# Residual updates in two token halves, weight casts ordered after the put-backs, and a rotary key of 128 rows in a one-layer FFN, mixer and FFN kernel

## The chip, the cores and the metric

The kernel runs on one core of a Trainium2 chip. The metric is device time in microseconds (us), lower is better. Engines are named as the profile names them: PE (TensorE matmul) and PEld (its weight loads), DVE (VectorE), ACT (ScalarE), POOL (GpSimd) and SP (SyncE, whose queue issues nearly all DMAs).

## The reference, cut

One encoder layer in float32 on 256 tokens of width 2048. D_FF is 5632; the attention has 8 heads, with 128 columns of a head's own key and a rotary key of 64 columns that all heads share.

```python
mod = silu(c) @ w_ada + b_ada                      # nine vectors: shift, scale, gate, three times
n = rms(h, ffn1_norm) * (1 + sc1) + sh1
h = h + 0.5 * g1 * ((silu(n @ w_gate) * (n @ w_up)) @ w_down)          # FFN 1
n = rms(h, mix_norm) * (1 + sc2) + sh2
proj = n @ w_in                                    # u, v, c_q, c_kv, k_pe
a = gmlp_mixer(u, v)
m = mla_mixer(c_q, c_kv, k_pe)                     # scores = q_nope . k_nope + q_pe . k_pe
h = h + g2 * (concat[rms(a), rms(m)] @ w_out)      # mix
n = rms(h, ffn2_norm) * (1 + sc3) + sh3
h = h + 0.5 * g3 * ((silu(n @ w_gate) * (n @ w_up)) @ w_down)          # FFN 2
h = rms(h, final_norm)
```

## The kernel before

**Weights.** Every weight matrix comes through `split`: one DMA of 128 x 2048 into a `raw` tile; then, for each of its two halves, ACT copies a rounded high part `whi` (128x1024, L170) and DVE subtracts it to form the low part `wlo` (L174). The matmuls (all of them are recorded at L121, in the helper `mm`) take hi x hi, hi x lo and lo x hi products, where activations are split alike (`nh`, `nl`). One step is one `raw` tile: for each half of it 8 matmuls with `whi` and 4 with `wlo`, 24 in all, over two PSUM banks of 128 tokens x 512 columns, one bank for each half of the tokens. There are buffers for five raw tiles and for four hi and four lo halves.

**FFN.** `ffn` runs a first part (12 column groups `pg`, each with gate and up columns) and a second part, each followed by its down projection. In the first part the rows of the contraction are taken in passes: FFN 1 in row groups of 3, 3, 3, 3 and 4 tiles (`grouped`), FFN 2 in passes of two, one and one blocks (`in_passes`). Between passes the partial sums of a column group are copied out of PSUM by ACT (`keep_part`, L362), and at its next pass put back into two fresh banks by ACT (`take_part`, L366), which I call the put-back. After the last pass ACT and DVE form silu(g) * u (`th` at L326, `sg` and `a` at L327 and L328); four PE transposes (`tps`, L239) flip it, ordered after the last matmul of a step; ACT (L350) and DVE (L351) write the hi and lo parts of `s`.

**Order.** The kernel is written in program order, and each engine works through its own queue in the order in which the code issues; a helper `tc.issue_after` puts what stands in its block behind a named instruction, and where it isn't used, a scheduler settles the order of independent work. `run` begins step i+1 (`begin`: new banks, put-back, `split`) while the matmuls of step i are written.

**Down projection and boundaries.** Four column blocks c of 512 columns. At the end of a block `add_out` multiplies the two banks by the gate row (L290), adds the product to the residual `h` (L291), and `TokenNorm.add` sums squares on ACT (L252). `gate_row` forms the gate of 512 columns by four transposes (`tpg`) and an ACT copy (L284), once in each column block during the first half of an FFN. After the last block `TokenNorm.done` reduces the sums (L259), keeps PE going with matmuls called `idle`, and takes the root by a power on POOL (L182); `make` then normalizes (`hn`, L268), transposes (`tpn`) and writes the hi and lo parts of `n` (L276 to L278) for the next stage. The same stands behind the mixer's out projection. At the end the output is written by four DMAs of 512 columns for all tokens (L1011).

**Scores.** The rotary key `kpeT` holds the same 64 rows twice, at rows 0 and 64; `scores` takes for each head the 64 rows that its query stands in.

Of the kernel before, what the change touches and what calls it, by code (L numbers as in the profile page):

```python
# [17 lines left out]
P = 128  # L18
D = 2048
# [51 lines left out]
def encoder_layer(ctx: ExitStack, tc: tile.TileContext, outx, *, xT, x, pos, cst, vnorm, w_ada, gu1k, gu1, dn1a,  # L71
# [171 lines left out]
    class TokenNorm:  # L243


        def __init__(self):
            self.ss = stat(8)

        def add(self, c):
            for t in range(2):  # L250
                sq = tmp.tile([P, 512], F32, tag="hn", bufs=2, name="sq")
                act.activation(sq, h[:, t, c * 512 : c * 512 + 512], AF.Square, scale=1.0 / math.sqrt(D),  # L252
                               accum_out=self.ss[:, t * 4 + c : t * 4 + c + 1])

        def done(self, warm=False):
            ss = stat(2)
            if warm:
                keep_warm(mark["gu"], 6)
            dve.tensor_reduce(ss, self.ss.rearrange("p (t c) -> p t c", t=2), axis=AX.X, op=ALU.add)  # L259
            if warm:  # L260
                idle = bank("aux", "idle")
                keep_warm(mm(idle[:, :2], ident, ss, True, True), 6)
            self.r = rstd(ss, 2)

        def make(self, n, d0, sh, gs):
            hn = tmp.tile([P, 2, T], F32, tag="hn", bufs=2, name="hn")
            for t in range(2):
                dve.tensor_scalar(hn[:, t], h[:, t, d0 * P : d0 * P + T], self.r[:, t : t + 1], None, op0=ALU.mult)  # L268
            ps = bank("aux", "tpn")
            flip4(ps, lambda j, t: hn[:, t, j * P : j * P + P])  # L270
            for j in range(2):
                d = d0 + j
                nr = tmp.tile([P, T], F32, tag="nr", name="nr")
                s, g = mods[:, sh, d : d + 1], mods[:, gs, d : d + 1]
                o = ps[:, j * T : j * T + T]
                act.activation(n[0][:, d], o, AF.Identity, bias=s, scale=g)  # L276
                dve.tensor_scalar(nr, o, g, s, op0=ALU.mult, op1=ALU.add)  # L277
                dve.tensor_tensor(n[1][:, d], nr, n[0][:, d].bitcast(F32), op=ALU.subtract)  # L278

    def gate_row(m, c, g):  # L280
# [5 lines left out]
    def add_out(banks, c, g, norm=None):  # L286
        sl = slice(c * 512, c * 512 + 512)
        for t in range(2):
            e = tmp.tile([P, 512], F32, tag="hn", bufs=2, name="e")
            dve.tensor_tensor(e, banks[t], g, op=ALU.mult)  # L290
            dve.tensor_tensor(h[:, t, sl], h[:, t, sl], e, op=ALU.add)  # L291
        if norm:
            norm.add(c)
# [10 lines left out]
    def wide(w, banks, xs, first, last):  # L304

        half = (len(xs) + 1) // 2
        for i, ((whi, wlo), x) in enumerate(zip(w, (xs[:half], xs[half:]))):
            hi, lo = (y.rearrange("p (k c) -> p k c", k=len(x)) for y in (whi, wlo))
            for k, (a, b) in enumerate(x):
                for t in range(2):  # L310
                    mm(banks[t], a[:, token(t)], hi[:, k], first and i == 0 and k == 0, False)
                    mm(banks[t], b[:, token(t)], hi[:, k], False, False)
            for k, (a, _) in enumerate(x):
                for t in range(2):
# [3 lines left out]
    def gu_chunk(w, banks, n, kt0, nk, first, last):  # L318
        wide(w, banks, [(n[0][:, kt], n[1][:, kt]) for kt in range(kt0, kt0 + nk)], first, last)
# [11 lines left out]
    def ffn(gu, dn, n, gate, ada_pg, ada_dn, lead, groups, prep, norm, before_down=None):  # L331
        with tc.tile_pool(name="actp", bufs=1) as actp, tc.tile_pool(name="ftmp", bufs=2) as ftmp:
# [3 lines left out]
            grow = ftmp.tile([P, 4, 512], F32, bufs=1, name="grow")  # L336
# [31 lines left out]
            def run(steps, part, slots):  # L368
# [14 lines left out]
                for i, (pg, kt0, nk, opens, load, more) in enumerate(steps):  # L383
                    gu_chunk(w, banks, n, kt0, nk, kt0 == 0, kt0 + nk == KT)
# [10 lines left out]
            def in_passes(slots):  # L395
                def load(pg, kg):
# [4 lines left out]
                     for kgs in PASSES for pg in range(FIRST) for kg in kgs], {}, slots)  # L401
# [48 lines left out]
            for half in range(2):  # L450
# [5 lines left out]
                kqs = len(slots) // 4  # L456
                for c in range(4):
                    banks = [bank("acc" if c % 2 else "aux", "dn") for _ in range(2)]
                    for kq in range(kqs):
                        if half == 0 and before_down:  # L460
# [3 lines left out]
                        wide(w, banks, slots[kq * 4 : kq * 4 + 4], kq == 0, kq == kqs - 1)  # L464
# [63 lines left out]
    rb1 = tmp.tile([P, T], F32, bufs=1, name="rb1")  # L528
# [50 lines left out]
    ffn(gu1, (dn1a, dn1b), n1, G1, ADA_UP1, ADA_DOWN1, gu1k, [gu1g[f"gu1_{g}"] for g in range(len(GROUPS))], prep1, norm, gate_cols(G1))  # L579
# [3 lines left out]
    norm2.done(True)  # L583
    n2 = new_n()
    with tc.tile_pool(name="mix", bufs=1) as mix:
        u = mix.tile([P, 2, 1024], F32, name="u")
        vg = mix.tile([P, 2, 1024], F32, name="vg")
        cqT = mix.tile([P, 2, 4, T], F32R, tag="cm", name="cqT")
        ckvT = [mix.tile([P, 2, T], F32R, tag="qT", bufs=2, name="ckvT") for _ in range(2)]
        kpeT = mix.tile([P, T], F32, name="kpeT")  # L590
# [6 lines left out]
        def a_form(w, banks, lhs, kts, first, last):  # L597
            per = len(kts) // 2
            for half in range(2):
                hi, lo = (x.rearrange("p (k c) -> p k c", k=per) for x in w[half])  # L600
                ks = kts[half * per : half * per + per]
                for i, kt in enumerate(ks):
                    for t in range(2):
# [3 lines left out]
                for i, kt in enumerate(ks):  # L607
                    for t in range(2):
# [3 lines left out]
        def proj(i, kg, banks, n_ada, prep=False):  # L612
            if prep:
                for d in (kg * 4, kg * 4 + 2):
                    norm2.make(n2, d, SH2, SC2)
            w = split(win_a[i, kg])
            ada(n_ada)
            a_form(w, banks, n2, list(range(kg * 4, kg * 4 + 4)), kg == 0, kg == 3)
# [18 lines left out]
        def rotate(dst, x, heads):  # L637
# [3 lines left out]
            ps = tmp.tile([P, 4, 64 * heads], F32, tag="hn", bufs=2, name="ps")  # L641
            p1, p2, p3, p4 = (ps[:, i].rearrange("p (t a b) -> p t a b", t=2, a=heads) for i in range(4))
# [57 lines left out]
        for kg in range(4):  # L700
            proj(1, kg, banks, ADA_MIX["v0"][kg])
            if kg == 1:
# [3 lines left out]
                act.copy(kpeT, ps[:, :T])  # L706
# [154 lines left out]
        def a_flip():  # L861
            mA = nslot.tile([P, KT, T], F32R, tag="nl", name="mA")
            transpose_split(u, 8, (mA[:, :8], mA[:, 8:]), "out_norm_gmlp")
            return mA
# [5 lines left out]
        def scores(g, j):  # L870
            rows = slice(64 * j, 64 * j + 64)
# [34 lines left out]
        def out_pair(part, i, m, norm=None):  # L906
# [3 lines left out]
            if kq == 0:  # L910
                held[0] = [bank("acc", "wo") for _ in range(2)]
                held[1] = mix.tile([P, 512], F32, tag="grow", name="grow")
                gate_row(G2, c, held[1])
            ks = range(kq * 4, kq * 4 + 4)
            wide(w, held[0], [(m[:, k], m[:, 8 + k]) for k in ks], kq == 0, kq == 1)
            if kq:
                add_out(held[0], c, held[1], norm)
# [32 lines left out]
        mM = nslot.tile([P, KT, T], F32R, tag="nh", name="mM")  # L950
        for k in range(8):
# [3 lines left out]
            act.activation(mM[:, k], hr, AF.Identity, scale=g)  # L955
            dve.scalar_tensor_tensor(mM[:, 8 + k], hr, g, mM[:, k].bitcast(F32), op0=ALU.mult, op1=ALU.subtract)
        out_pair(0, 6, mA)
        out_pair(0, 7, mA)
        norm = TokenNorm()
        for dp in range(8):  # L960
# [5 lines left out]
    norm3.done(True)  # L966
    n3 = new_n()
# [8 lines left out]
    def prep3(kg, pg):  # L976
        if pg == 0 and kg < cut:
            for d in (kg * 4, kg * 4 + 2):
                norm3.make(n3, d, SH3, SC3)
        for m, d in ahead3.get((kg, pg), ()):  # L980
            mod_col(m, d, 1, True)
            if m == SH3:
                mod_end(SC3, d, d + 1, "scale", "ffn2_norm")
                mod_end(SH3, d, d + 1, "shift")
                if d % 2:
                    norm3.make(n3, d - 1, SH3, SC3)

    norm = TokenNorm()
    ffn(gu2, (dn2a, dn2b), n3, G3, none, (none, none), None, None, prep3, norm, gate_cols(G3))


    fn = const.tile([P, D], F32, tag="cb", name="fn")
    sync.dma_start(fn, fnorm)
    with tc.tile_pool(name="fin", bufs=1) as fin:
        o = fin.tile([P, 2, D], F32, name="o")
        for c in range(3):
            for t in range(2):
                sl = slice(c * 512, c * 512 + 512)
                dve.tensor_tensor(h[:, t, sl], h[:, t, sl], fn[:, sl], op=ALU.mult)
        norm.done()  # L1000
        for c in (3, 0, 1, 2):
            sl = slice(c * 512, c * 512 + 512)
            for t in range(2):
                r = norm.r[:, t : t + 1]
                if c == 3:
                    dve.scalar_tensor_tensor(o[:, t, sl], h[:, t, sl], r, fn[:, sl], op0=ALU.mult, op1=ALU.mult)
                elif c == 0 or (c == 1 and t == 0):
                    act.activation(o[:, t, sl], h[:, t, sl], AF.Identity, scale=r)
                else:
                    dve.tensor_scalar(o[:, t, sl], h[:, t, sl], r, None, op0=ALU.mult)  # L1010
            sync.dma_start(outx[:, :, sl], o[:, :, sl])  # L1011
# [93 lines left out]
```

## Time and profile before

| | |
|---|---|
| runs | 1840.97 us median of 3 (1837.91 to 1841.42) |
| the profiled execution | 1839.86 us, of which the span (first to last instruction) 1838.1 us |
| PE busy | 1788.3 us, 97% of the span |
| PEld / DVE / ACT / POOL busy | 1474.0 / 1329.1 / 964.8 / 29.4 us |
| mean granted TensorE clock | 0.989 of full speed |
| read from memory | 480.01 MB, 262 GB/s over the span |

A busy time is the sum of an engine's instructions; matmuls overlap in the pipeline, so the time from one start to the next is shorter than a record's own length (0.39 us for a matmul that starts 0.23 after the one before it). The releaser of a wait is the instruction that came last among those waited for.

### The profile page before, as it was taken

What the parts mean: (1) busy time and instruction counts of PE and PEld (TensorE: products, weight loads), DVE (VectorE), ACT (ScalarE), POOL (GpSimd) and SP (SyncE); (2) the same over time, 40 slices, a digit from 0 to 9 for tenths busy, and PEclk for the clock granted to TensorE, in tenths of its full rate; (3) what the DMA queues carried; (4) which work ended last, traced back from release to release, by engine and by line L of the source; (5) the groups of instructions that cost most, each with busy time, mean ns of one, the idle gap of its engine ahead of it and who ended that gap; (6) DMA issues with size and microseconds to landing.
All of it is one profiled execution on the core that took longest, in us unless ns stands there. A gap on an engine that the chain in (4) does not pass through costs nothing.

```text
span 1838.1 us, 21587 instructions
## 1 busy us (share of the span) xinstructions
PE 1788.3 (97%) x8078; PEld 1474.0 (80%) x8078; DVE 1329.1 (72%) x1730; ACT 964.8 (52%) x1456; POOL 29.4 (2%) x25
## 2 busy tenths in 40 slices
PE   6999999999999999999999999999999999999996
PEld 4788777888888888888877878888778888888885
DVE  7888878887777778696877886666687855555554
ACT  3788865343444444366675544467654334444442
POOL 1000000000000000001010000000000000000000
PEclk7999999999999999999999999999999999999998
DMA  8989975988778878757856567777568865555551
GB/s 335 332 317 328 339 284 223 356 352 317 301 277 304 311 298 312 286 209 276 313 177 225 192 243 297 261 296 268 181 248 309 320 245 186 196 191 183 183 206 46
DMA packets 70681, 483.52 MB, mean 263 GB/s; under 512 B 7856, under 2 KB 8112, under 8 KB 17584
## 3 DMA queue, kind: packets, MB, share of 16 engines
q1 hardware_dynamic: 70576, 482.14, 71.0%
q8 instruction: 63, 1.03, 0.2%
q14 instruction: 42, 0.34, 0.0%
HBM read 480.01 MB, written 2.10 MB: 262 GB/s over the span
## 4 chain that ended last, share of the span: by engine, by line
PE 54%; issue 41%; DVE 2%; ACT 2%; DMA 0%; POOL 0%; SPq 0%; POOLq 0%; DVEq 0%; ACTq 0%
PE gu L121 25%; PE dn L121 13%; PE wo L121 4%; PE u L121 2%; PE v L121 2%; PE cq L121 1%; PE sc L121 1%; ACT whi L170 1%; DVE ada L132 1%; PE ckv L121 1%; PE qproj L121 1%; DVE wlo L174 0%; PE av L121 0%; DMA xt<-in_xT_dram 0%; PE tpg L239 0%
## 5 line engine op out<-in xcount | busy, mean ns | idle before, releaser
L174 DVE TENSOR_TENSOR wlo<-raw,whi 128x1024 fp32r<-128x1024 f32 (+2 forms) x639 | 747.9, 1181 | 420.4 <-ACT whi L170 415.1
L170 ACT CAST whi<-raw 128x1024 fp32r<-128x1024 f32 (+2 forms) x642 | 648.8, 1019 | 717.2 <-PE gu L121 377.4
L121 PE MATMUL gu<-whi,nh 128*128 128x512 f32 x1408 | 556.2, 395 | 18.3 <-ACT whi L170 12.7
L121 PE MATMUL gu<-whi,nl 128*128 128x512 f32 x1408 | 552.4, 393 | 0.3 <-DVE nl L278 0.3
L121 PE MATMUL gu<-wlo,nh 128*128 128x512 f32 x1408 | 385.1, 391 | 0.0
L121 PE MATMUL dn<-whi,s 128*128 128x512 f32 x1408 | 349.4, 391 | 0.0
L121 PEld LDWEIGHTS gu<-whi,nh 128*128 128x128 f32 x1408 | 266.0, 189 | 79.0 <-ACT whi L170 14.8
L132 DVE CUSTOM_DVE_ANT_0 ada<-ada,cb 128x2048 f32<-128x2048 f32 (+1 forms) x144 | 322.7, 2242 | 0.0
L121 PEld LDWEIGHTS gu<-wlo,nh 128*128 128x128 f32 x1408 | 266.0, 189 | 55.7
L121 PEld LDWEIGHTS gu<-whi,nl 128*128 128x128 f32 x1408 | 266.4, 189 | 54.7 <-DVE nl L278 0.7
L121 PEld LDWEIGHTS dn<-whi,s 128*128 128x128 f32 x1408 | 263.4, 188 | 54.0
L121 PE MATMUL dn<-wlo,s 128*128 128x512 f32 x704 | 188.3, 390 | 0.0
L121 PEld LDWEIGHTS dn<-wlo,s 128*128 128x128 f32 x704 | 132.2, 188 | 27.4
L362 ACT COPY p<-gu 128x512 f32<-128x512 f32 x144 | 77.4, 588 | 30.2 <-PE gu L121 29.9
L366 ACT COPY gu<-p 128x512 f32<-128x512 f32 x144 | 82.3, 598 | 0.4 <-DVE nr L277 0.4
L182 POOL TENSOR_TENSOR stats<-stats,half_m 128x2 f32<-128x2 f32 (+2 forms) x13 | 19.3, 1484 | 1704.9 <-DVE stats L181 1704.9
L290 DVE TENSOR_TENSOR e<-dn,grow 128x512 f32<-128x512 f32 x32 | 20.6, 686 | 20.8 <-PE dn L121 20.8
L121 PE MATMUL wo<-whi,mA 128*128 128x512 f32 x128 | 34.4, 402 | 0.0
L327 DVE SCALAR_TENSOR_TENSOR sg<-th,gu 128x256 f32<-128x256 f32 x88 | 32.9, 416 | 0.3 <-ACT th L326 0.3
L328 DVE TENSOR_TENSOR a<-sg,gu 128x256 f32<-128x256 f32 x88 | 32.9, 416 | 0.0
L121 PE MATMUL wo<-whi,mM 128*128 128x512 f32 x128 | 32.1, 393 | 0.0
L351 DVE TENSOR_TENSOR s<-tps,s 128x512 fp32r<-128x512 f32 x44 | 30.2, 686 | 2.0 <-ACT s L350 2.0
(214 smaller groups left out, 1102.8 us busy)
## 6 DMA issues: line engine op xcount, KB each, us to landing
ada<-in_w_ada_dram SPq DMA_DIRECT2D x144, 1024.0 KB, 5.2
raw<-in_gu_dram SPq DMA_DIRECT2D x140, 1024.0 KB, 4.8
raw<-in_gu_dram SPq DMA_DIRECT2D x44, 768.0 KB, 5.9
raw<-in_dn1a_dram SPq DMA_DIRECT2D x24, 1024.0 KB, 5.4
raw<-in_dn2a_dram SPq DMA_DIRECT2D x24, 1024.0 KB, 5.1
raw<-in_dn1b_dram SPq DMA_DIRECT2D x20, 1024.0 KB, 5.5
raw<-in_win_a_dram SPq DMA_DIRECT2D x20, 1024.0 KB, 6.0
raw<-in_dn2b_dram SPq DMA_DIRECT2D x20, 1024.0 KB, 4.7
```

The lines of the kernel that those rows point to most:

```text
L121: return pe.matmul(out, w, x, start=start, stop=stop, skip_group_check=True)
L132: dve.tensor_tensor_reduce(out=w[:, sl], in0=w[:, sl], in1=cb[:, sl], scale=0.5, scalar=acc if i else 0.0, op0=ALU.mult, op1=ALU.add, accu ...
L170: mark["act"] = act.copy(hi, raw[:, a:b])
L174: mark["dve"] = dve.tensor_tensor(lo, raw[:, a:b], hi.bitcast(F32), op=ALU.subtract)
L182: pool.tensor_tensor(r, ss, half_m[:, :n], op=ALU.pow)
L290: dve.tensor_tensor(e, banks[t], g, op=ALU.mult)
L327: dve.scalar_tensor_tensor(s, th, 1.0, g, op0=ALU.add, op1=ALU.mult)
L328: dve.tensor_tensor(a, s, u, op=ALU.mult)
L351: dve.tensor_tensor(lo, ps, hi.bitcast(F32), op=ALU.subtract)
L362: act.copy(part[pg][:, t], banks[t])
L366: act.copy(banks[t], part[pg][:, t])
```

## The change

- **Casts.** `take_part` now returns its last put-back copy, and in `begin` the `split` of a step with a put-back is issued after that copy.
- **Boundaries.** In the last column block before a norm, the last step of the contraction runs all its matmuls for token half 0, then for half 1 (`end_columns`); after each half come its residual update, square sum, root and the first four column tiles of the next stage's `n` (`lead`). The first step of the next stage also runs half 0 first.
- **Output.** The final norm does the same for each token half; its gain is loaded earlier, and each half is written by two DMAs of 1024 columns.
- **Rotary key.** `kpeT` has two copies of 128 rows, one with the key in rows 0 to 63 and zeros below, one the other way round; all score matmuls have 128 rows.
- **Gate rows and buffers.** The gate row is formed in both halves of an FFN, in a buffer for one row; the product of bank and gate is written back in PSUM, and so is the Square's unused result.

```diff
     class TokenNorm:
...
+        def add(self, c, t, scratch):
+            act.activation(scratch, h[:, t, c * 512 : c * 512 + 512], AF.Square, scale=1.0 / math.sqrt(D),
+                           accum_out=self.ss[:, t * 4 + c : t * 4 + c + 1])
+        def root(self, t):
+            ss = stat(1)
+            dve.tensor_reduce(ss, self.ss[:, 4 * t : 4 * t + 4], axis=AX.X, op=ALU.add)
+            self.r[t] = rstd(ss, 1)
...
+        def lead(self, t, sh, gs):
+            self.root(t)
+            hn = tmp.tile([P, 4, P], F32, tag="hn", name="hn")
+            dve.tensor_scalar(hn.rearrange("p a b -> p (a b)"), h[:, t, :512], self.r[t], None, op0=ALU.mult)
+            ps = bank("aux", "tpl")
+            flip4(ps, lambda j, i: hn[:, 2 * j + i])
+            for d in range(4):
+                self.parts(ps[:, d * P : d * P + P], d, sh, gs, token(t))
...
+    def add_out(banks, c, g, norm=None, ts=(0, 1)):
         sl = slice(c * 512, c * 512 + 512)
+        for t in ts:
+            dve.tensor_tensor(banks[t], banks[t], g, op=ALU.mult)
+            dve.tensor_tensor(h[:, t, sl], h[:, t, sl], banks[t], op=ALU.add)
+            if norm:
+                norm.add(c, t, banks[t])
+    def end_columns(w, banks, xs, first, c, g, norm, lead):
+        if norm is None or c < 3:
+            wide(w, banks, xs, first, True)
+            add_out(banks, c, g, norm)
+            return
         for t in range(2):
+            wide(w, banks, xs, first, True, (t,))
+            add_out(banks, c, g, norm, (t,))
+            lead(t)
+        if norm.n:
+            keep_warm(mark["gu"], 6)
...
             def take_part(part, pg, banks):
                 for t in range(2):
-                    act.copy(banks[t], part[pg][:, t])
+                    last = act.copy(banks[t], part[pg][:, t])
+                return last
...
                     if opens and kt0:
                         new = [bank(tag(pg), "gu") for _ in range(2)]
-                        take_part(part, pg, new)
-                    w = load()
+                        with tc.issue_after(take_part(part, pg, new).ins):
+                            w = load()
+                    else:
+                        w = load()
...
+                        if kq == (0 if half else 4):
+                            g = gate_row(gate, c)
...
-                        if half == 0 and kq == 4:
-                            gate_row(gate, c, grow[:, c])
-                    add_out(banks, c, grow[:, c], norm if half else None)
...
-                act.copy(kpeT, ps[:, :T])
+                for j in range(2):
+                    pool.memset(kpeT[64 - 64 * j : 128 - 64 * j, j], 0.0)
+                    act.copy(kpeT[64 * j : 64 * j + 64, j], ps[64 * j : 64 * j + 64, :T])
...
-                mm(o, qrt[rows, t * P : t * P + P], kpeT[rows], False, True)
+                mm(o, qrt[:, t * P : t * P + P], kpeT[:, j], False, True)
...
+        def lead(self, t):
+            self.root(t)
+            r = self.r[t]
+            for c in (0, 3, 1, 2):
...
+            for c in range(2):
+                sync.dma_start(outx[:, t, c * 1024 : c * 1024 + 1024], self.o[:, t, c * 1024 : c * 1024 + 1024])
```

The order of ACT in the last pass of FFN 1's first part, before, one step and the start of the next. `p6` is the kept partial sum of a column group, `gu_2339` and `gu_2340` are the banks that PE fills next, with `whi_2345` and `whi_2349`, which stand seven rows further up, a step earlier; `whi_2403` and `whi_2407` are for the step after that:

```order
L170 CAST whi_2403<-raw_2401 128x1024
L170 CAST whi_2407<-raw_2401 128x1024
L366 COPY gu_2339<-p6_1824 128x512
L350 CAST s4_2307<-tps_2332 128x512
L366 COPY gu_2340<-p6_1824 128x512
L326 ACTIVATE th_2353<-gu_2281 128x256
L326 ACTIVATE th_2359<-gu_2282 128x256
```

The same place in the changed kernel, where `gu_2338` and `gu_2339` are the banks that PE fills next, with `whi_2344` and `whi_2348`:

```order
L356 ACTIVATE th_2352<-gu_2280 128x256
L395 COPY gu_2338<-p6_1823 128x512
L379 CAST s4_2306<-tps_2331 128x512
L395 COPY gu_2339<-p6_1823 128x512
L170 CAST whi_2344<-raw_2342 128x1024
L170 CAST whi_2348<-raw_2342 128x1024
L356 ACTIVATE th_2358<-gu_2281 128x256
```

The casts of the step that PE starts next have moved from a step ahead of the put-backs to right behind them, and the first `th` of the step before has moved ahead of the put-backs.

PE at the end of FFN 1 and the first projection (`cq`), before; `dn` are down matmuls, `idle` those that keep PE going:

```order
L121 MATMUL dn<-whi,s_5319 128x512 x8
L121 MATMUL dn<-wlo,s_5319 128x512 x4
L121 MATMUL idle<-cb,cs_74 128x128 x6
L121 MATMUL idle<-stats,cs_74 128x2
L121 MATMUL idle<-cb,cs_74 128x128 x6
L239 MATMUL tpn<-cs_74,hn 128x128 x9
L121 MATMUL cq<-whi,nh 128x512 x2
```

The same place in the changed kernel; `tpl` are the transposes of `lead`:

```order
L121 MATMUL dn<-whi,s_5165 128x512 x4
L121 MATMUL dn<-wlo,s_5165 128x512 x2
L121 MATMUL dn<-whi,s_5314 128x512 x4
L121 MATMUL dn<-wlo,s_5314 128x512 x2
L239 MATMUL tpl<-cs_74,hn 128x128 x4
L121 MATMUL cq<-whi,nh 128x512
L121 MATMUL cq<-whi,nl 128x512
L121 MATMUL cq<-whi,nh 128x512
L239 MATMUL tpl<-cs_74,hn 128x128 x4
L121 MATMUL idle<-cb,cs_74 128x128 x6
```

The down matmuls of the last step shown are those of token half 1; the transposes of half 0 come right behind them, and those of half 1 behind three matmuls of the projection.

POOL in the changed kernel, from the last of the startup's weight halves on:

```order
L172 TENSOR_TENSOR wlo_270<-raw_263,whi_269 128x1024
L747 MEMSET kpeT_6170 64x256 x2
L182 TENSOR_TENSOR stats_78<-stats_78,half_m_81 128x1 x2
L182 TENSOR_TENSOR stats_78<-stats_78,half_m_81 128x2
L182 TENSOR_TENSOR stats_78<-stats_78,half_m_81 128x4
```

The two memsets of the rotary key have come in ahead of the roots of the first boundary, which are now two of 128x1.

## Rows read from the trace of the kernel before

**Rows 1.** The page's first part: busy us, share of the span, instructions.

```profile
PE 1788.3 (97%) x8078; PEld 1474.0 (80%) x8078; DVE 1329.1 (72%) x1730; ACT 964.8 (52%) x1456; POOL 29.4 (2%) x25
```

**Rows 2.** The chain of waits, 296 to 304 us: start, length, engine and line.

```profile
296.34 1.06 ACT whi L170
297.39 0.49 ACT gu L366
...
302.78 1.05 ACT whi L170
```

**Rows 3.** Timeline of one put-back step: start, length, engine, line, operation, count, [idle before].

```profile
1300.29 1.08 PE L121 MATMUL gu<-wlo,nh 128*128 128x512 f32 x4
...
1300.49 1.06 ACT L170 CAST whi<-raw 128x1024 fp32r<-128x1024 f32 x1 [1.44 <-PE gu L121]
...
1301.20 0.60 PE L239 MATMUL tps<-cs,a 128*128 128x128 f32 x4
1301.44 0.58 ACT L366 COPY gu<-p 128x512 f32<-128x512 f32 x1
1301.58 1.22 DVE L174 TENSOR_TENSOR wlo<-raw,whi 128x1024 fp32r<-128x1024 f32 x1 [1.28 <-ACT whi L170]
1301.96 0.58 ACT L350 CAST s<-tps 128x512 fp32r<-128x512 f32 x1
...
1302.08 0.50 PE L121 MATMUL gu<-whi,nh 128*128 128x512 f32 x1 [0.27 <-ACT gu L366]
...
1302.44 0.59 ACT L366 COPY gu<-p 128x512 f32<-128x512 f32 x1
...
1302.96 0.66 ACT L326 ACTIVATE th<-gu 128x256 f32<-128x256 f32 x2
```

**Rows 4.** Groups of ACT by line, 244 to 310 us: count, busy us, mean ns, idle.

```profile
L366 ACT COPY gu<-p 128x512 f32<-128x512 f32 x20 | 11.7, 584 | 0.0
```

**Rows 5.** Stretches of 3.4 us: busy us by engine, then granted PE clock, DMA.

```profile
79.80:83.20 3.40, 3.33 (x8) 2.66 (x9) 2.68 (x3) 3.40 (x7) 0.00 (x0) 0.50 0.61 187
...
219.70:223.10 3.40, 3.40 (x17) 2.82 (x16) 3.27 (x4) 2.64 (x6) 0.00 (x0) 1.00 0.68 205
```

**Rows 6.** Timeline of PE at the idle time ahead of those two stretches.

```profile
79.87 0.80 PE L121 MATMUL gu<-whi,nh 128*128 128x512 f32 x1 [2.28 <-ACT whi L170]
...
218.13 0.50 PE L121 MATMUL gu<-whi,nh 128*128 128x512 f32 x1 [1.79 <-ACT whi L170]
```

**Rows 7.** Timeline of PE at a gate row in the down projection.

```profile
338.11 0.60 PE L239 MATMUL tpg<-cs,mods 128*128 128x128 f32 x4
...
338.46 1.40 PE L121 MATMUL dn<-whi,s 128*128 128x512 f32 x5
```

**Rows 8.** Timeline of the scores' matmuls and weight loads (PEld).

```profile
949.17 0.70 PE L121 MATMUL sc<-kpeT,qrT 64*128 64x256 f32 x2
...
949.80 0.30 PEld L121 LDWEIGHTS sc<-kT,qT 128*128 128x128 f32 x2 [0.33 <-issue]
949.80 0.70 PE L121 MATMUL sc<-kT,qT 128*128 128x256 f32 x2
...
965.55 0.60 PE L121 MATMUL sc<-kT,qT 128*128 128x256 f32 x2
```

**Rows 9.** The scores' tile: count, shortest, median and longest ns, first and last start.

```profile
L121 PE MATMUL sc<-kT,qT x32: 377/380/484, 948.6 to 1010.0; 128*128 128x256 f32 x32
```

**Rows 10.** Timeline from the last down matmuls of FFN 1 to the first projection.

```profile
773.66 1.07 PE L121 MATMUL dn<-wlo,s 128*128 128x512 f32 x4
...
778.96 0.70 POOL L182 TENSOR_TENSOR stats<-stats,half_m 128x2 f32<-128x2 f32 x1 [733.83 <-DVE stats L181]
...
782.13 1.07 PE L121 MATMUL cq<-whi,nh 128*128 128x512 f32 x2
```

**Rows 11.** Timeline of the end, from the last down matmuls of FFN 2.

```profile
1822.96 1.07 PE L121 MATMUL dn<-wlo,s 128*128 128x512 f32 x4
...
1827.58 0.69 POOL L182 TENSOR_TENSOR stats<-stats,half_m 128x2 f32<-128x2 f32 x1 [746.08 <-DVE stats L181]
...
1829.66 3.52 SPq L1011 DMA_DIRECT2D out_dram<-o  x4
```

More of the change, by code (lines that the diff above doesn't have):

```diff
@@ L247, in __init__, with open, more, parts @@
             self.ss = stat(8)
-        def add(self, c):
-            for t in range(2):
[L251 to L268, printed above, removed]
+            self.r = [None, None]
+            self.n = None
+        def open(self):
+            self.n = new_n()
+        def more(self, c):
+            pass
+        def add(self, c, t, scratch):
[5 more added lines that the diff above has]
+            self.r[t] = rstd(ss, 1)
+        def parts(self, o, d, sh, gs, at):
+            nr = tmp.tile([P, T], F32, tag="nr", name="nr")[:, at]
+            s, g = mods[:, sh, d : d + 1], mods[:, gs, d : d + 1]
+            hi, lo = self.n[0][:, d, at], self.n[1][:, d, at]
+            act.activation(hi, o, AF.Identity, bias=s, scale=g)
+            dve.tensor_scalar(nr, o, g, s, op0=ALU.mult, op1=ALU.add)
+            dve.tensor_tensor(lo, nr, hi.bitcast(F32), op=ALU.subtract)
+        def make(self, d0, sh, gs):
+            hn = tmp.tile([P, 2, T], F32, tag="hn", name="hn")
+            for t in range(2):
+                dve.tensor_scalar(hn[:, t], h[:, t, d0 * P : d0 * P + T], self.r[t], None, op0=ALU.mult)
             ps = bank("aux", "tpn")
@@ L301, in make_n, with wide @@
         dve.scalar_tensor_tensor(lo, nr, s, hi.bitcast(F32), op0=ALU.add, op1=ALU.subtract)
-    def wide(w, banks, xs, first, last):
+    def wide(w, banks, xs, first, last, ts=(0, 1)):
         half = (len(xs) + 1) // 2
@@ L309, in wide @@
             for k, (a, b) in enumerate(x):
-                for t in range(2):
+                for t in ts:
                     mm(banks[t], a[:, token(t)], hi[:, k], first and i == 0 and k == 0, False)
@@ L329, in swiglu, with ffn @@
         return a
-    def ffn(gu, dn, n, gate, ada_pg, ada_dn, lead, groups, prep, norm, before_down=None):
+    def ffn(gu, dn, n, gate, ada_pg, ada_dn, lead, groups, prep, norm, before_down, root):
         with tc.tile_pool(name="actp", bufs=1) as actp, tc.tile_pool(name="ftmp", bufs=2) as ftmp:
@@ L365, in take_part, with run @@
                 for t in range(2):
-                    act.copy(banks[t], part[pg][:, t])
-            def run(steps, part, slots):
+                    last = act.copy(banks[t], part[pg][:, t])
+                return last
+            def run(steps, part, slots, apart=False):
                 def begin(pg, kt0, nk, opens, load, more):
@@ L459, in ffn @@
                     for kq in range(kqs):
-                        if half == 0 and before_down:
+                        if half == 0:
                             before_down(c, kq)
@@ L595, in pair, with a_form @@
             return [bank(tag, name)[:, :n] for _ in range(2)]
-        def a_form(w, banks, lhs, kts, first, last):
+        def a_form(w, banks, lhs, kts, first, last, ts=(0, 1)):
             per = len(kts) // 2
@@ L602, in a_form @@
                 for i, kt in enumerate(ks):
-                    for t in range(2):
+                    for t in ts:
                         tok = slice(t * P, t * P + P)
@@ L607, in a_form @@
                 for i, kt in enumerate(ks):
-                    for t in range(2):
+                    for t in ts:
                         mark["pe"] = mm(banks[t], lhs[0][:, kt, t * P : t * P + P], lo[:, i], False,
@@ L959, in encoder_layer @@
         norm = TokenNorm()
+        norm.open()
         for dp in range(8):
@@ L976, in prep3 @@
     def prep3(kg, pg):
-        if pg == 0 and kg < cut:
-            for d in (kg * 4, kg * 4 + 2):
-                norm3.make(n3, d, SH3, SC3)
+        if pg == 0 and kg == 1:
+            for d in range(4, EARLY, 2):
+                norm3.make(d, SH3, SC3)
         for m, d in ahead3.get((kg, pg), ()):
@@ L985, in prep3 @@
                 if d % 2:
[L986 to L1001, printed above, removed]
+                    norm3.make(d - 1, SH3, SC3)
```

110 lines of the change are left out of this document (59 added, 51 removed).

## The prediction

> **What bounds the kernel now.** I read the engines' busy time first: PE is busy for 97% of the span [rows 1], so time is lost or won only where PE stands still, runs at the lower clock, or has its work shortened. The chain of waits then shows where PE does stand still. In the last pass over an FFN's first half it leaves PE once a step: cast, put-back, then PE, again and again [rows 2]. One turn is 302.78 - 296.34 = 6.44 us, of which 24 matmuls of 0.227 us are 5.45. The timeline of one step [rows 3] is the pattern of 10 such steps in each FFN (20 put-backs in the stretch 244 to 310 are 10 pairs, [rows 4]). The last lo matmul's slot ends at X = 1300.29 + 4 x 0.227 = 1301.20; four transposes follow on PE; the first put-back starts at X + 0.24 and ends at X + 0.82; PE goes on at X + 0.88. So PE sits for only 0.27 us behind its transposes. The cover is that ACT's two casts for the next step ran a step earlier: one starts at 1300.49, before X.
>
> **The change part by part.** The run behind the profile took 1839.9 us, its span being 1838.1; it lies 1.1 below the median of the runs, and I add to 1839.9.
>
> *Casts tied to the put-backs.* In the order of the changed kernel each of these 20 steps has on ACT: th of bank 0, put-back, cast of s, put-back, **both weight casts of the step that PE starts next**, then th of bank 1. ACT works in that order, so the casts that used to be a step ahead now stand between PE and its next matmul. Lengths and spacings are those of [rows 3]. th of bank 0 needs the third of the four lo matmuls, starting X - 0.46; an engine that waits for a matmul starts 0.43 after that matmul's start (last transpose 1301.53, s at 1301.96), which makes X - 0.03. Two th take 0.66, so one takes 0.33: first put-back X + 0.30; s 0.52 later, X + 0.82 (its transposes are ready at X + 0.76); second put-back 0.48 later, X + 1.30; first cast 0.52 later, X + 1.82 to X + 2.88. PE restarts 0.06 later, at X + 2.93 in place of X + 0.88. That is 2.05 us a step, **+41 us** for 20. The second cast and the two lo halves follow in time: the second cast ends at X + 3.93, VectorE's 1.22 us for each lo end near X + 4.1 and X + 5.2, and PE asks for them at X + 4.7 and X + 7.5. Queued behind the casts are th of bank 1 and with it the product that the next transposes need, but those come only at the step's end. The bounds are narrow since every duration has a row: 1.8 to 2.3 a step, +36 to +46.
>
> *What the gap does to TensorE's clock.* The transposes end at X + 0.60, so PE now idles 2.33 us in each of these steps, where it idled 0.27. The trace has idle stretches of that size: after 2.28 us the granted clock was 0.50 (1.2 GHz) for 3.4 us, after 1.79 it stayed at 1.00 [rows 5, 6]. In 3.4 us at half clock PE does 1.7 us of work. If each of 20 gaps brings this, it is +34; if none, 0. 2.33 is nearest to the 2.28 that lowered it, but by little, and some gaps may pass: I take five in six, **+28**.
>
> A page speaks against this term. The Trainium skill (TensorE: Matmul & The Clock Gate, "HAM oscillation — how this bites in real kernels") lets the clock fall only after idle gaps clearly longer than any that I expect here; by it the 28 us vanish, and rival 1 is the result. The row with 2.28 us does not agree with it in this kernel, so the row decides.
>
> *Rotary key in 128 rows.* A score matmul starts every 0.315 us on average (949.17 to 949.80 are two), as a weight load waits 0.33 at each change between 64 and 128 rows; within a pair of equal height the second starts 0.60 - 0.38 = 0.22 after the first [rows 8, 9]. There are 32 of each kind, so 64 x 0.095 = 6.1 us at most. Zeros fill the other 64 rows, so no matmul grows. Some of the gain goes back to the softmax that these steps feed: **-4.5** (-6 to 0). The two memsets for the zeros are under the boundary.
>
> The Trainium skill (TensorE: Matmul & The Clock Gate, "The mechanism" of row and column tiling) has a weight load overlap matmuls in flight only where the row groups differ; by it full height would gain nothing and the term be 0. Here the second load of a pair of equal height waits for nothing and the waits stand where heights change [rows 8], so the row decides.
>
> *Gate rows.* The FFNs now form the gate row in both halves, 24 in place of 16. Four transposes cost PE 338.46 - 338.11 = 0.35 us between down matmuls [rows 7]: 8 x 0.35 = **+2.8** (0 to +6, if the copy also holds a cast back).
>
> *Boundaries in two token halves.* Last down matmul to first projection matmul is 782.13 - (773.66 + 0.91) = 7.56 us [rows 10]. Afterwards token half 0 has its residual, square sum, root and first four columns made under the 12 matmuls of half 1 (2.7 us), and the first matmuls of half 0 can begin some 3 us earlier. But the chain of half 1 starts no sooner than before, and stands behind half 0's work on VectorE. PE does 12 matmuls earlier and then waits for the rest. I take **-1** for both boundaries together; ends are -4 and +4.
>
> *Tail.* From the last matmul's slot (1822.96 + 0.91 = 1823.87) to the span's end are 14.2 us; the first output transfer goes out 5.8 us into it, after the root at 1827.58 [rows 11]. Half 0's residual, root and outputs now come under half 1's 12 matmuls and its chain, so half the output leaves earlier; half 1 queues behind half 0's output operations. **-2.2** (-3 to -1).
>
> Put in place at no cost: residual products written into PSUM and the Square's scratch there are as many instructions of the same size; the root's POOL operation for each half is beside the other half's matmuls, and costs its 0.7 us if that cover is gone.
>
> Sum: 1839.9 + 41 + 28 - 4.5 + 2.8 - 1 - 2.2 = **1904 us**.
>
> **The rivals.** *1: the clock holds in these gaps.* For it speaks that 1.79 us left it alone and that 2.28 is a single row with a lower clock after a gap between like matmuls; against it, that 2.33 is longer than that. Time 1904 - 28 = 1876. *2: the tie does what its words say, and the put-backs move into ACT's idle time before X.* ACT is idle 1.44 us before its cast [rows 3]; with put-backs there PE would lose no 0.44 a step, 20 x 0.44 = 8.8 us: 1839.9 - 8.8 - 4.5 + 2.8 - 1 - 2.2 = 1826, faster. It decides at the point where put-backs and a cast (2.6 us on ACT) are over by X, thus where th of bank 0 starts before X - 2.9; the order puts th ahead of them, and th needs the step's end, which is why I give it little. *3: the boundary turns worse.* The two memsets of 64x256 stand on POOL ahead of the first root after the first FFN. No row has this operation; bounds are 0.1 us (the smallest operations) and the 0.70 of the root's own operation [rows 10] for 64 rows, up to some 2.5 us each if POOL writes slowly; then the first projection waits 5 us more and no boundary gains: about 1910. *4: casts come later but ACT or the bank releases cancel the gains exactly*: within 0.2% of 1840.
>
> **How the numbers follow.** Forecast 0.68, rival 1 0.17, rival 3 0.07, rival 2 0.05, rival 4 0.03. The predicted time is the forecast's 1904. Its own ends: the steps at +36 to +46, clock 15 to 34, so some 1886 to 1916. To hold 8 in 10 the range takes in rival 3 and the upper part of rival 1: 1874 to 1915. Something below 0.2% could not be told from no change by a measurement; faster by more than that is rival 2, 0.05; within it 0.03; slower 0.92.
>
> **What would show it.** Right: in the last pass of both FFNs' first halves the chain is th, put-back, s, put-back, cast, PE at 8.4 to 10.2 us a step; PE's idle before the first matmul of a step is 2.2 to 2.5 us and its releaser the cast, not the put-back; the granted clock in those two stretches is well under 0.99 on average; the score loads wait no more. Wrong: the casts run a step ahead in the trace, or steps stay near 6.4 us; or the clock there stays 1.00 (rival 1); or the POOL memsets hold the root.

## The result, and the profile after

The changed kernel takes **1905.16 us** (median of 4 runs, 1902.37 to 1906.47) against 1840.88 us for the kernel before (median of 4): a ratio of 1.0351, 95% interval 1.0333 to 1.0369. It is slower by 64 us; 1904 had been forecast. The span of the profiled run is 1904.7 us at a mean granted clock of 0.973, where it was 1838.1 at 0.989.

The page's first part, after: busy us, share of the span, instructions. PE now has 90 us in which it does nothing, where it had 50 [rows 1], and its own busy time has grown by 27 us although its matmuls are nearly the same.

```profile
PE 1814.9 (95%) x8082; PEld 1496.9 (79%) x8082; DVE 1335.7 (70%) x1747; ACT 968.3 (51%) x1474; POOL 30.9 (2%) x30
```

The timeline of one step of the last pass, after (start, length, engine, line, operation, count, [idle before <- releaser]). It is the step of [rows 3].

```profile
1336.94 1.08 PE L121 MATMUL gu<-wlo,nh 128*128 128x512 f32 x4
1337.82 0.38 ACT L356 ACTIVATE th<-gu 128x256 f32<-128x256 f32 x1 [5.89 <-PE gu L121]
1337.86 0.60 PE L239 MATMUL tps<-cs,a 128*128 128x128 f32 x4
1338.10 0.59 ACT L395 COPY gu<-p 128x512 f32<-128x512 f32 x1
...
1338.61 0.59 ACT L379 CAST s<-tps 128x512 fp32r<-128x512 f32 x1
...
1339.09 0.60 ACT L395 COPY gu<-p 128x512 f32<-128x512 f32 x1
...
1339.61 2.00 ACT L170 CAST whi<-raw 128x1024 fp32r<-128x1024 f32 x2
...
1340.71 0.69 PE L121 MATMUL gu<-whi,nh 128*128 128x512 f32 x1 [2.26 <-ACT whi L170]
```

X, the end of the last matmul's slot, is 1337.85. Every row of ACT stands where the prediction put it to within 0.06 us (th X - 0.03, put-backs X + 0.25 and X + 1.24, cast X + 1.76), and PE restarts at X + 2.86 against a forecast of X + 2.93. Its releaser is the cast, no longer the put-back. The group rows for the stretch 244 to 344 us (count | busy us, mean ns | idle before, releaser) show that it is so in all 10 steps: 22.6 us of PE's idle time, and ACT itself idle for 55.4 us ahead of `th`, whereas it had waited ahead of the casts.

```profile
L121 PE MATMUL gu<-whi,nh 128*128 128x512 f32 x83 | 38.8, 467 | 22.6 <-ACT whi L170 22.6
```

```profile
L356 ACT ACTIVATE th<-gu 128x256 f32<-128x256 f32 x21 | 8.1, 386 | 55.4 <-PE gu L121 55.4
L395 ACT COPY gu<-p 128x512 f32<-128x512 f32 x20 | 11.9, 596 | 0.0
```

The clock, in a timeline of PE behind one of these gaps: matmuls start 0.43 us apart at first (1.2 GHz), and 0.23 later in the step (2.4 GHz).

```profile
296.17 0.64 PE L121 MATMUL gu<-whi,nh 128*128 128x512 f32 x1 [2.27 <-ACT whi L170]
296.61 0.63 PE L121 MATMUL gu<-whi,nl 128*128 128x512 f32 x1
297.04 0.63 PE L121 MATMUL gu<-whi,nh 128*128 128x512 f32 x1
...
300.85 0.39 PE L121 MATMUL gu<-whi,nl 128*128 128x512 f32 x1
301.08 0.39 PE L121 MATMUL gu<-whi,nh 128*128 128x512 f32 x1
```

From the end of one step's transposes to the next there are 8.44 us in three of the 20 steps and 9.97 to 10.09 in the other 17; before it was 6.45. Over two stretches of 100 us that hold most of the steps the mean granted clock (the third number from the end) is 0.87 and 0.85, where before it was 1.00 from 240 to 340:

```profile
240.00:340.00 100.00, 77.37 (x295) 60.69 (x294) 48.44 (x75) 43.84 (x75) 0.00 (x0) 0.87 0.38 133
1325.00:1425.00 100.00, 77.37 (x287) 60.52 (x286) 47.19 (x70) 43.37 (x73) 0.00 (x0) 0.85 0.28 96
```

Where the rest went, read from the starts of matmuls in the two traces:

| stretch | before | after | difference |
|---|---|---|---|
| first part of FFN 1 (first matmul to first down matmul) | 289.48 | 323.69 | +34.2 |
| down projections and second part of FFN 1 | 464.04 | 466.12 | +2.1 |
| boundary 1 and the first projection (to the first `v` matmul) | 50.10 | 52.14 | +2.0 |
| scores (first to last) | 62.07 | 56.27 | -5.8 |
| last out matmul to the first down matmul of FFN 2 | 283.67 | 319.66 | +36.0 |
| down projections and second part of FFN 2 | 464.06 | 466.11 | +2.1 |
| last down matmul to the end of the span | 14.5 | 11.5 | -3.0 |

### The profile page after: what moved, and what is told of

Read it like the earlier page. It is cut to its first block, busy times and chain, and to the rows that moved or that the text cites. A ratio compares the mean times of both kernels' runs of the same rounds, so it can differ in the third digit from the quotient of the medians.

```text
span 1904.7 us, 21543 instructions
## 1 busy us (share of the span) xinstructions
PE 1814.9 (95%) x8082; PEld 1496.9 (79%) x8082; DVE 1335.7 (70%) x1747; ACT 968.3 (51%) x1474; POOL 30.9 (2%) x30
## 5 line engine op out<-in xcount | busy, mean ns | idle before, releaser
L121 PE MATMUL gu<-whi,nh 128*128 128x512 f32 x1408 | 568.1, 404 | 59.6 <-ACT whi L170 59.0
L121 PE MATMUL gu<-whi,nl 128*128 128x512 f32 x1408 | 563.9, 401 | 0.0
L121 PE MATMUL gu<-wlo,nh 128*128 128x512 f32 x1408 | 390.7, 397 | 0.0
L121 PEld LDWEIGHTS gu<-whi,nh 128*128 128x128 f32 x1408 | 272.5, 194 | 123.4 <-ACT whi L170 65.8
L121 PEld LDWEIGHTS gu<-wlo,nh 128*128 128x128 f32 x1408 | 273.0, 194 | 59.1
L121 PEld LDWEIGHTS gu<-whi,nl 128*128 128x128 f32 x1408 | 273.1, 194 | 57.2 <-DVE nl L273 0.5
L356 ACT ACTIVATE th<-gu 128x256 f32<-128x256 f32 x88 | 31.0, 380 | 122.9 <-PE gu L121 122.9
L182 POOL TENSOR_TENSOR stats<-stats,half_m 128x1 f32<-128x1 f32 (+3 forms) x16 | 20.2, 1265 | 1012.4 <-DVE stats L181 1012.4
L305 DVE TENSOR_TENSOR dn<-dn,grow 128x512 f32<-128x512 f32 x32 | 20.9, 695 | 20.2 <-PE dn L121 20.2
```

Of the source, the lines that this page charges most:

```text
L121: return pe.matmul(out, w, x, start=start, stop=stop, skip_group_check=True)
L182: pool.tensor_tensor(r, ss, half_m[:, :n], op=ALU.pow)
L305: dve.tensor_tensor(banks[t], banks[t], g, op=ALU.mult)
L356: act.activation(th, g, AF.Tanh, scale=0.5)
```

## The experiments

**The tie undone, all else kept.**

```diff
-                        with tc.issue_after(take_part(part, pg, new).ins):
-                            w = load()
-                    else:
-                        w = load()
+                        take_part(part, pg, new)
+                    w = load()
```

> The changed kernel with the tie of the casts undone, all else kept. Theory (the tie costs 20 gaps of PE and most of them the clock): in the trace after the change 20 gaps are 2.43 us where they were 0.44, so 20 x 1.99 = 39.8, and 17 to 18 of 20 steps ran 1.6 to 1.7 us longer at the lower clock, about 29; so 1905.2 - 39.8 - 29 = about 1836, steps of 6.4 us and a clock of 1.00 there; below the kernel before by some 4 to 5 us. Rival (the loss is spread over the tie and the other parts, which take from each other): 1845 to 1880.

Measured 1837.97 us (11 runs), ratio to before 0.9989 (0.9981 to 0.9998). Steps are 6.45 us again and the clock in them 1.00. So the tie alone costs 1905.2 - 1838.0 = 67.2 us, and all the rest of the change together gains about 1 us, less than the 4 to 5 that I had expected.

**The tie alone, in the kernel before.**

> The kernel before with the tie of the casts alone. Theory: the same 20 gaps and lowered clock, 1840.9 + 39.8 + 29 = about 1909, between 1905 and 1914. Rival (the gaps need the other parts too, through their buffers and banks): under 1890.

Measured 1906.96 us, ratio 1.0364 (1.0348 to 1.0380): +67.8 over the 1839.2 of before in the same comparison, with 17 of 20 steps at 10.0 us and three at 8.44, as in the changed kernel. It needs none of the other parts.

**Work for PE in the gaps.**

```diff
                         with tc.issue_after(take_part(part, pg, new).ins):
                             w = load()
+                        if kt0 + nk == KT and pg > 1:
+                            for _ in range(4):
+                                mm(new[0][:, :T], zero.to_broadcast([P, P]), cb[:, :T], False, False)
```

> The changed kernel with four matmuls in each of the 20 gaps that add zeros to the bank just put back (about 1.7 us of PE work, while the casts run); the casts stay where they are. Theory that the clock falls because PE idles: the gaps stay 2.4 us but the clock stays 1.00, so 1905.2 - 29 = about 1876, steps of 8.4 us. Rival (the clock is not the cause of the steps over 8.4 us, or falls for another reason): 1900 to 1910, steps of 10 us.

Measured 1877.16 us (1876.49 to 1879.26), 28.0 less than the change, with the casts where they were. All 20 steps take 8.42 to 8.45 us. Timeline of one of them; the matmuls that add zeros fill the gap while ACT casts:

```profile
1321.37 0.60 PE L241 MATMUL tps<-cs,a 128*128 128x128 f32 x4
1321.61 0.59 ACT L397 COPY gu<-p 128x512 f32<-128x512 f32 x1
...
1322.26 1.99 PE L123 MATMUL gu<-cb,zero 128*128 128x256 f32 x8 [0.29 <-ACT gu L397]
...
1323.12 2.00 ACT L172 CAST whi<-raw 128x1024 fp32r<-128x1024 f32 x2
```

Granted clock there (third number from the end):

```profile
1300.00:1385.00 85.00, 82.36 (x365) 64.72 (x364) 44.27 (x67) 40.39 (x70) 0.00 (x0) 1.00 0.34 121
```

The step's length for data, 8.44, is thus one thing, and the 1.6 us on top another, which goes when PE has work in the gap: 20 x (8.44 - 6.45) = 39.8 and 17 x 1.62 = 27.5 are the 67.3 that the tie costs.

**Only the second cast tied.** In `split` the copy of the second half alone stands behind the put-backs.

> The changed kernel with only the second of the two casts of a step tied behind the put-backs; the first stays a step ahead. Theory (PE waits for the first cast, the second has 2.7 us to spare): PE restarts after the first put-back, at X + 0.9, steps of 6.5 us, clock 1.00, within 2 us of the run without the tie: 1836 to 1839. Rival (what counts is that ACT is loaded with th, put-backs and a cast after X, whichever cast): 1.0 us a step or more, 1856 and above.

Measured 1838.96 us, ratio 0.9997 (0.9988 to 1.0006); steps of 6.47 to 6.49 us. ACT has the same load behind X, but PE waits only for the put-back:

```profile
1300.91 0.39 ACT L362 ACTIVATE th<-gu 128x256 f32<-128x256 f32 x1 [2.40 <-PE gu L121]
...
1301.19 0.59 ACT L401 COPY gu<-p 128x512 f32<-128x512 f32 x1
...
1301.84 0.50 PE L121 MATMUL gu<-whi,nh 128*128 128x512 f32 x1 [0.29 <-ACT gu L401]
...
1302.70 1.06 ACT L174 CAST whi<-raw 128x1024 fp32r<-128x1024 f32 x1
```

What costs the time is the first cast, whose lead of one step the tie takes away, and not the amount of work on ACT.

**The idle matmuls at the boundaries left out** (the `keep_warm` of `end_columns`), without the tie.

> The run without the tie (1838.0 us), and without the six idle matmuls that stand on PE behind each boundary's second transposes. They take 784.52 to 786.68 = 2.2 us there. If they are on the path: -2.2 for each of two boundaries, 1833.6. Rival (VectorE, which forms the lo parts of the half tiles until 788.6, is the bound there, so PE would wait anyway): within 1 us of 1838.

Measured 1836.59 us, ratio 0.9981 (0.9973 to 0.9990), some 1.4 us less than the run without the tie. In the traces boundary 1 is 1.05 us shorter and boundary 2 1.26, about half of the 2.2 that they take. At boundary 1 the first matmul behind their place starts 2.3 us earlier, seen from the last down matmul, but the tenth projection matmul only 1.4: the granted clock stays at 0.50 until 788.1, and the work that has moved forward runs at it. Some 40 us behind the down matmuls PE then waits 1.24 us for a `wlo`. Neither expectation holds as a whole.

**Casts behind half 1's chain**, without the tie.

```diff
-            w = split(win_a[i, kg])
+            w = late(win_a[i, kg]) if prep and kg == 1 else split(win_a[i, kg])
...
+    def late(src):
+        with tc.issue_after(mark["sq"].ins), tc.issue_after(mark["hn"].ins):
+            return split(src)
```

> The run without the tie (1838.0 us), with the weight casts and lo halves of the next stage's second step put behind half 1's square sum (ACT) and behind half 1's normalization (VectorE). There the first root waits for a lo half of 1.22 us (its POOL operation takes 1.38 in place of 0.54) and half 1's residual waits behind it. If that chain is the path: first projection 2 to 3 us earlier at each boundary, 1832 to 1834. Rival (VectorE is full there, and what is put behind is only done later): within 1 us of 1838. The POOL operation of the first root should fall to about 0.55 either way.

Measured 1834.90 us, ratio 0.9972 (0.9962 to 0.9983): 3.1 us less by the medians, 1.7 (boundary 1) and 0.4 (boundary 2) less in the traces. What the casts had done is plain in the timeline of boundary 1 in the run without the tie:

```profile
777.45 1.22 DVE L174 TENSOR_TENSOR wlo<-raw,whi 128x1024 fp32r<-128x1024 f32 x1
777.69 1.38 POOL L182 TENSOR_TENSOR stats<-stats,half_m 128x1 f32<-128x1 f32 x1 [0.63 <-DVE stats L181]
...
779.11 0.49 DVE L288 TENSOR_SCALAR hn<-h,stats 128x512 f32<-128x512 f32 x1 [0.44 <-POOL stats L182]
779.51 0.68 DVE L306 TENSOR_TENSOR h<-h,dn 128x512 f32<-128x512 f32 x1
```

The root takes 1.38 us on POOL and ends 0.40 after VectorE's lo half; half 1's residual then stands behind half 0's normalization. With the casts put back, the same operation in the same place:

```profile
775.85 0.54 POOL L182 TENSOR_TENSOR stats<-stats,half_m 128x1 f32<-128x1 f32 x1 [730.08 <-DVE stats L181]
...
776.43 0.61 DVE L288 TENSOR_SCALAR hn<-h,stats 128x512 f32<-128x512 f32 x1 [0.66 <-POOL stats L182]
```

**Gate rows once**, in four buffers, without the tie.

> The run without the tie (1838.0 us), with the gate rows formed only in an FFN's first half, kept in four buffers as in the kernel before. In the trace each FFN's down projections come 2.06 us later than before by their end: -4.1 us, 1833.9. Rival (the time of these 32 transposes is hidden, and the 2 us come from other work): 1837 to 1838.

Measured 1835.03 us, ratio 0.9973 (0.9962 to 0.9985): 2.9 us less by the medians, and each FFN's down projections and second part 2.07 us shorter in the trace, which is all that they had gained in length.

**64 rows of the key again**, without the tie.

> The run without the tie (1838.0 us), with score matmuls that take 64 rows of the key and the query again. The scores' stretch is 5.8 us shorter in the trace with 128 rows, all 64 matmuls starting 0.216 us apart; if the height is the reason: +5.8, 1843.8, with weight loads waiting 0.33 again. Rival (something else in the stage was shortened): within 1 us of 1838.

Measured 1843.88 us, ratio 1.0021 (1.0012 to 1.0030): +5.9. PE's timeline with 64 rows, then with 128:

```profile
952.34 0.70 PE L121 MATMUL sc<-kT,qT 128*128 128x256 f32 x2
952.97 0.70 PE L121 MATMUL sc<-kpeT,qrT 64*128 64x256 f32 x2
953.60 0.70 PE L121 MATMUL sc<-kT,qT 128*128 128x256 f32 x2
```

```profile
952.70 0.59 PE L121 MATMUL sc<-kT,qT 128*128 128x256 f32 x2
953.14 0.59 PE L121 MATMUL sc<-kpeT,qrT 128*128 128x256 f32 x2
953.57 0.59 PE L121 MATMUL sc<-kT,qT 128*128 128x256 f32 x2
```

Two matmuls take 0.63 us where the height changes, 0.43 where it doesn't; the weight load at a change has waited 0.33.

**The next step's banks before the transposes' bank**, without the tie. In program order the banks of a step are taken from the pool behind the bank of the transposes, which wait for the step before to end. On ACT the first put-back stands right behind a weight cast that has itself waited 1.44 us for PE [rows 3], and it is the same without the tie. The exchange moves both, the request for the banks and the place of the put-backs on ACT, and no run separates the two.

```diff
-                    if not opens or nk == 4:
-                        turn()
                     old = banks
                     if i + 1 < len(steps):
                         w, banks = begin(*steps[i + 1])
+                    if not opens or nk == 4:
+                        turn()
```

> The run without the tie (1838.0 us), with two lines of the loop over steps exchanged: the banks of the next step are taken and filled (put-backs, casts) before the bank of the transposes is taken. On ACT both put-backs and both casts then stand ahead of th of the step before, a whole step early. Theory (a put-back was late because its banks were handed out behind the bank of transposes that wait for the step's last matmul): PE's 0.27 us idle and the rest of the 0.44 a step vanish, 20 x 0.44 = -8.8: 1829. Rival (PE then waits for the casts or for th in another place): 1836 to 1840.

Measured 1828.18 us, ratio 0.9935 (0.9923 to 0.9948): 9.8 us less than without the tie. Steps are 5.91 to 5.94 us, and the group rows of PE (244 to 310 us) have no idle time left where [rows 3] had 0.27 us a step:

```profile
L121 PE MATMUL gu<-whi,nh 128*128 128x512 f32 x82 | 32.9, 401 | 0.0
```

The timeline of one step shows PE going on behind its transposes without a wait, and the put-backs after that, so that they are for the step behind this one. They stand behind `th` and `s` on ACT, where I had expected them ahead of `th`.

```profile
1301.05 0.60 PE L239 MATMUL tps<-cs,a 128*128 128x128 f32 x4
1301.29 0.64 ACT L356 ACTIVATE th<-gu 128x256 f32<-128x256 f32 x2
...
1301.40 0.48 PE L121 MATMUL gu<-whi,nh 128*128 128x512 f32 x1
...
1302.29 0.61 ACT L395 COPY gu<-p 128x512 f32<-128x512 f32 x1
...
1303.28 0.59 ACT L395 COPY gu<-p 128x512 f32<-128x512 f32 x1 [0.38 <-DVE s L380]
```

**The whole change, tie included, with this exchange.**

> The whole change, the tie included, with the exchange alone: banks of the next step taken and put back before the bank of the transposes. Theory (the tie costs only because the put-backs it ties the casts to come after the step's last matmul; where they come a step early the casts are tied to something early): as the run with the exchange and no tie, 1828, steps of 6.0 us, clock 1.00. Rival (the tie itself takes away the step of lead that the casts need): above 1850.

Measured 1828.62 us, ratio 0.9933 (0.9919 to 0.9946), steps of 5.91 to 5.94 us: as without the tie. The granted clock, again the third number from the end:

```profile
245.00:305.00 60.00, 60.00 (x285) 49.61 (x284) 46.61 (x76) 39.90 (x67) 0.00 (x0) 1.00 0.64 230
```

So the tie is harmless as soon as what it ties the casts to comes early. Two lines take 76.5 us off the changed kernel.

**The four repairs together**: gate rows once, casts put back, no idle matmuls, and at the end half 1's residual ahead of half 0's output operations on VectorE.

> The run without the tie (1838.0 us), with gate rows formed once (about -3 to -4), casts behind half 1's square sum and normalization (-2 to -3), no idle matmuls (-1 to -2), and at the end half 1's residual ahead of half 0's output operations on VectorE, where it stood 1.5 us behind them (-1.5). If the four add up: 1827 to 1830. Rival (they share one wait, so that the sum is less): 1831 to 1834.

Measured 1832.40 us (1829.75 to 1838.83), ratio 0.9969 (0.9958 to 0.9980), and so only 5.6 below the run without the tie. By stages of the traces the gate rows give their 4.1 and the end 1.3, but the two boundaries together 2.2 (1.5 and 0.8), no more than either of the two repairs there gave alone (2.3 and 2.2). That these two share one wait fits this, but is not shown. (The spans of the two traces differ by 6.6, the start of the kernel being 1.0 us longer in this one.) Differences of 1 to 3 us are better read from the stages than from the medians: the first part of FFN 1, which these repairs leave alone, takes 287.9 to 290.6 us in the traces of the runs with neither the tie nor the exchange.

**All of it with the exchange.**

> All of the run before this one, and the exchange. The exchange acts in the FFNs' last passes and the others at boundaries, down projections and the end, so they should add: 1829 less 8.8 = about 1820. Rival (the earlier put-backs shift ACT's work into the casts' time): 1826 or more.

Measured **1823.05 us** (1819.60 to 1825.85), ratio 0.9907 (0.9894 to 0.9921): 0.9% faster than before. The exchange adds 9.4 to the four repairs, as it had given 9.8 without them.

## Why the prediction was right, step by step

| step | predicted | measured | from |
|---|---|---|---|
| casts behind the put-backs | +41 | +39.8 | 20 x (8.44 - 6.45) |
| clock in the gaps | +28 | +27.5 | 17 steps longer by 1.62; 28.0 with the gaps filled |
| rotary key | -4.5 | -5.8 | the scores' stretch; 5.9 by the run with 64 rows |
| gate rows | +2.8 | +4.1 | twice 2.07 |
| boundaries | -1 | +3 | run without the tie: +1.6 and +1.4 against before |
| tail | -2.2 | -3.0 | 14.5 to 11.5 |
| sum | +64 | +66 | the rows above; 1904.7 - 1838.1 = 66.6 by the spans |

**The main step** held in its mechanism, place and size. It rested on two readings: that ACT's order, and not ACT's load, decides (the run with the second cast alone tied shows this), and that the length of every operation between X and PE's restart had a row. The 1.99 us a step instead of 2.05 are the 0.06 by which ACT ran ahead, since the first put-back started 0.28 us behind `th` and not 0.33.

**The clock** was the uncertain term, and rival 1 the case without it. Both are decided: the gaps alone make 1877, and idle PE the other 28. That five in six gaps would lower it was an estimate from one row of 2.28 us; 17 of 20 did it, at 2.26 to 2.27; that the share came out so near is luck. The page of the Trainium skill that the prediction weighed (TensorE: Matmul & The Clock Gate, "HAM oscillation — how this bites in real kernels") would have let the clock hold; the measurement goes against it here, and which three gaps of the same length pass is not explained by anything in these runs.

**Rotary key:** the full 64 x 0.095 = 6.1 came nearly whole. The step that failed is the discount for the softmax: at most 0.3 us was handed back, where 1.6 had been taken off.

**Gate rows:** the row that I read for four transposes, 0.35 us, ends at the start of the next matmul, but the four behind that one came late too, by 0.10 us together (five matmuls in 1.40 us [rows 7], where 4 x 0.227 + 0.39 = 1.30): eight rows cost 4.1, half a us each.

**Boundaries:** the sign was wrong, inside the ends given. I had counted half 0's earlier start (it came: from start to start the first projection matmul is 5.0 us behind the last down matmul in place of 7.8) and half 1's chain behind it, but not the lo halves of the next weights, which fell between half 0's square sum and its root, nor the idle matmuls in front of ready work. In the run with the four repairs the boundaries come to 0.2 and 0.6 us above before, not below. What is left may be VectorE: a hi-and-lo pair costs it 0.41 + 0.29 us for a half tile of 128 tokens and 0.54 + 0.42 for a whole one, so that eight half tiles take 1.8 us more than four whole ones. No run took this by itself.

The clock is a second candidate, which the prediction had left out. Behind boundary 1 the granted clock was 0.50 for 3.4 us before (779.5 to 782.9) and for 6.8 us without the tie (779.6 to 786.4); boundary 2 is alike. The first row is the stretch right behind those 3.4 us before, the second the 6.8 us without the tie (the clock is the third number from the end):

```profile
782.90:786.30 3.40, 3.20 (x18) 2.37 (x17) 3.40 (x10) 2.25 (x5) 0.00 (x0) 1.00 0.00 0
779.60:786.40 6.80, 5.83 (x20) 4.29 (x21) 5.73 (x24) 3.25 (x8) 0.54 (x1) 0.50 0.50 192
```

What the clock can cost there is seen where the code is the same: with all repairs boundary 1 takes 50.3 us, and with the exchange added 51.7. In both traces four transposes start 15.2 us behind the last down matmul, with the same PE rows in the same order before and after them; there the clock falls a second time with the exchange, and matmuls start 0.43 us apart in place of 0.23. The same place without the exchange and with it:

```profile
790.20:793.60 3.40, 3.40 (x17) 2.61 (x16) 3.40 (x9) 2.65 (x5) 0.00 (x0) 1.00 0.00 0
786.20:789.60 3.40, 3.40 (x11) 2.67 (x10) 3.40 (x9) 2.58 (x4) 0.00 (x0) 0.50 0.00 0
```

How much of the +3 at the boundaries is VectorE's and how much the clock's stays open.

**The total** missed by 1 us, and that is luck in part: the boundaries came out 4 us worse than forecast and the gate rows 1.3, while the rotary key (1.3), the casts (1.2), the tail (0.8) and the clock (0.5) came out better.

**The other rivals.** Rival 2, put-backs in ACT's idle time, is not what the tie does; but the price put on it, 8.8 us, is what the exchange of two lines gained (9.8 and 9.4). Rival 3 named the memsets as the trap at boundary 1; they took 0.67 us together and were over before the root could start, so they held nothing; the operation in the root's way was VectorE's.

## What to carry to other kernels

Before an instruction is ordered behind another one, ask when that other one runs: a tie takes over all the waits of what it is tied to, and here the put-backs ran on ACT behind `th`, which waits for a step's last matmuls. A prefetch that leads by one step costs nothing until something puts it behind work of the current step; then PE waits for it, and for what stands ahead of it, in each step (1.99 us here), and most times pays again by the clock (1.62). Work in front of an idle engine is the thing to look for: of 67 us lost, 28 were recovered by matmuls that did nothing, and all of them by taking the next step's banks two lines earlier.

## What the runs showed of the hardware

Gaps of 2.26 us that come back every 8 to 10 us lowered PE's clock in 17 of 20 cases, 1.6 us each, and matmuls that fill them kept it at 1.00 in all 20 steps although they compute nothing. Two traces with the same code at a boundary can differ by 1.4 us because the clock fell a second time in one of them.

A POOL operation that takes 0.54 us took 1.38 (boundary 1) and 1.45 (boundary 2) when a VectorE subtraction of 1.22 us began before it, and ended 0.4 us after that; with the subtraction moved away it took 0.54 and 0.55. The Trainium skill (SBUF — State Buffer, "Who interferes with whom") says that VectorE and GpSimd share a pair of ports under an exclusive lock, and that a VectorE instruction with two inputs in SBUF, as this subtraction has, contends with a GpSimd instruction that reads SBUF. The trace agrees, with these numbers.

Weight loads waited 0.33 us where the number of rows changed between two matmuls, those of 128 rows behind 64 like those of 64 behind 128: 32 score matmuls with half their rows filled with zeros made 64 matmuls 5.8 us shorter.
